# Shifted weight units and another order of splits in a three-product float32 decoder trunk

## Chip, cores and metric

The kernel runs on one core of a Trainium2 chip. The metric is the device time of one execution in microseconds (us); lower is better.

## The reference

Two decoder layers work on one sequence of 512 tokens with 1024 channels. Each layer is a half-step SwiGLU block, a mixer (gated linear attention with pooling in layer 0, top-k attention in layer 1) and a second half-step SwiGLU block; a last norm follows. So there are four SwiGLU blocks, and they hold most of the arithmetic:

```python
def swiglu(x, wi, wo):
    gate, up = jnp.split(x @ wi, 2, axis=-1)
    return (jax.nn.silu(gate) * up) @ wo
...
for li in range(DEPTH):
    h = h + 0.5 * swiglu(rms_norm(h, ffn1_norm[li]), ffn1_wi[li], ffn1_wo[li])
    hn = rms_norm(h, mix_norm[li])
...
    h = h + mix
    h = h + 0.5 * swiglu(rms_norm(h, ffn2_norm[li]), ffn2_wi[li], ffn2_wo[li])
return rms_norm(h, final_norm)
```

Here `wi` is 1024 x 5632 and `wo` 2816 x 1024, all in float32.

## The kernel before

**Products.** Every float32 operand of a large product is split into a high part (a copy to the type fp32r, by ScalarE) and a low part (the rest, by VectorE). `mm3` (L277 to 281) then issues three matmuls for each pair of 128 x 128 weights and moving tile: high by high (L279), high by low and low by high. In the blocks the weights are the stationary operand and the activations move. Most products have 512 moving columns. In the blocks' "seven products" (`seven_products`, L596 to 674), a 2 x 2 block scheme with seven products in place of eight, they have 256: 12 matmuls to a product, 84 to one of the 22 column groups `f` of a block. Also of 256 columns are the mixers' value products (bank `v`, 288 matmuls in all, where the weights move and the activations are stationary) and the output product of the odd mixer (bank `oo`, 384).

**Blocks.** `ffn(i, ...)` (L384) runs block i = 0 to 3. Its first groups `f` (four in block 0, three in the others, table `PLAIN`) are plain products of 512 columns; the others are seven products. The 22 groups are cut into three thirds (`THIRDS`: 8, 7, 7); each third ends with an output stage over m = 0 to 7 (bank `o`, 512 columns, 3 x 7 or 3 x 8 matmuls to each m).

**Weights.** A weight chunk is loaded by SP's DMA queue into one of two buffers `src0` and `src1`, in turn (`emit_load`, L214), and is split from there into units. There are four units, each a pair of tiles `u0h, u0l` to `u3h, u3l`; a unit can be written again when the products that read it have ended. A plain chunk takes two units for its two halves. A chunk of seven products takes unit 0 for `ab`, unit 1 for `z` and unit 2 or 3 (in turn) for `ds`; VectorE first adds blocks of the raw chunk together (L682, L691, L693). In its products `ab` is read first, then `ds`, then `z`.

```python
def unit_tile(u, off, name):
    n = (UNIT if u < 2 else UNIT + S) + UPAD
    return tuple(wpool.tile([P, n], F32R, tag=f"u{u}{x}", name=f"u{x}_{name}")[:, off:n] for x in "hl")
```

`off` counts columns of 4 bytes: the unit's data begin `off` columns into its tile. The unit tiles begin 160 bytes past a multiple of 256, and the moving tiles of the blocks (`hgh`, `hgl`, `th`, `tl`) 96 bytes past one. With off = 48 (192 bytes) a unit therefore begins at 96 too, and moving and stationary tiles lie at a **distance** of 0 (moving address less stationary address, modulo 256 bytes); all products of 512 columns with weights stand at 0. The table `SHIFT` gives the seven products another `off` in each third of each block, so another distance:

| block | distance in its thirds (bytes) |
|---|---|
| 0 | 192, 160, 128 |
| 1 | 96, 64, 32 |
| 2 | 0, 224, 176 |
| 3 | 240, 208, 80 |

The `v` and `oo` products stand at 192.

**Order.** In `ffn` the work is recorded as tasks with an engine, an assumed duration and dependencies; `Schedule.run` (L94) plays them through and emits each engine's instructions in the order that comes out. PE and SP keep the order in which tasks were added; ScalarE and VectorE follow the assumed times. Each engine then works strictly through its list. Lines 406 to 410 stand for what is under way when a block begins: the loads of its third and fourth chunk land after 3 and 5 us, the first products wait 5 us (`begun`), and in block 0 VectorE is busy for 20 us. `load_up_to` takes a load for 2.4 us per 1024 columns.

Of the kernel before, what the change touches and what calls it, by code (L numbers as in the profile page):

```python
# [17 lines left out]
P = 128  # L18
# [6 lines left out]
THIRDS = ((0, 8), (8, 15), (15, 22))  # L25

PLAIN = ((0, 1, 2, 3), (0, 1, 2), (0, 1, 2), (0, 1, 2))

SHIFT = ((0, 8, 16), (24, 32, 40), (48, 56, 4), (52, 60, 28))
UNIT = 1024  # L30
UPAD = 64
RANK = 16
EPS = 1e-6
# [109 lines left out]
def trunk(ctx, tc, xT, pos, wi, wo, wev, walr, gw, pw, wevo, wod, wodx, wodo, cst, cident, cperm, cscan, clev, ccaus,  # L143
# [24 lines left out]
    def chunk(kind, src, n, eng=V, units=(0, 1), off=0):  # L168
        chunks.append((kind, src, n, eng, units, off))

    def ffn_chunks(i):
        for t, (fa, fb) in enumerate(THIRDS):
            for f in range(fa, fb):
                if f in PLAIN[i]:
                    chunk("P", wi[i, f], 2048, units=(2, 3) if f % 2 else (0, 1), off=48)
                else:
                    chunk("S", wi[i, f], 2048, off=SHIFT[i][t])
            for m in range(0, KD, 3):
                n = (fb - fa) * P
                c0 = fa * KD * P + m * n  # L180
                chunk("O", wo[i, :, c0:c0 + min(3, KD - m) * n], min(3, KD - m) * n)

    def mix_chunks(them):
        for n, (src, eng, off) in enumerate(them):
            chunk("C", src, src.shape[-1], eng, ((0, 1), (2, 3))[n % 2], off)

    ffn_chunks(0)
    EVEN0 = len(chunks)
    chunk("A", walr, KD * RANK)
    mix_chunks([(wev[c], G if c > 1 else V, 32 if c in (2, 3) else 48) for c in range(8)]  # L190
               + [(wevo[c], V if c > 1 else G, 0) for c in range(4)])
    ffn_chunks(1)
    ffn_chunks(2)
    mix_chunks([(wod[0], V, 48), (wodx, V, 48)]
               + [(wod[c], V if c == 6 else G, 32 if c == 6 else 48) for c in range(1, 7)]
               + [(wodo[c], V if c > 1 else G, 0) for c in range(4)])
    ffn_chunks(3)
    parts = {}
# [185 lines left out]
    def ffn(i, next_gain, rope_steps=None):  # L384
        last_ffn = next_gain is None
        with tc.tile_pool(name=f"ffn{i}", bufs=1) as fp, tc.tile_pool(name=f"ffnt{i}", bufs=2) as ft:
# [17 lines left out]


            for n in (2, 3):
                loaded[at["use"] + n] = add("SP", (3.0, 5.0)[n - 2], lambda: None)
            begun = add("SP2", 5.0, lambda: None)
            if i == 0:
                add("DVE", 20.0, lambda: None).late = -1.0  # L410


            def load_up_to(c):
                while at["load"] <= min(c, len(chunks) - 1):
                    n = at["load"]
                    loaded[n] = add("SP", 2.4 * chunks[n][2] / 1024, lambda n=n: emit_load(n), src_free[n % 2])
                    src_free[n % 2] = []
                    at["load"] += 1

# [139 lines left out]
            def plain_products(f, t, c, w, tls, rest):  # L559
                gp, up = new_bank("g"), new_bank("u")  # L560
                d = {"third": t}
                units = chunks[c][4]
                for q in range(4):
                    def mms(q=q):
                        w_ = w()
                        for k in (2 * q, 2 * q + 1):
                            for s, rec in enumerate((gp, up)):
                                mm3(ps_of(rec), col(w_, k * 256 + s * P, k * 256 + (s + 1) * P), hg[k],
                                    k == 0, k == KD - 1)
                    tp = add("PE", 12 * 0.2267, mms, tls[q // 2] if tls else None,  # L570
                             (gp["after"], up["after"]) if q == 0 else None, begun if f == 0 else None)
                    readers[units[q // 2]].append(tp)
                    if rest and q < 3:
                        rest.pop(0)()
                    if i == 0 and f == 1 and q == 1:
                        add_norm()
                if f == 0:
                    if i > 0:
                        add_norm()
                    add_blocks()  # L580

                def gate():
                    d["g"] = ft.tile([P, S], F32, tag="g", name=f"g{f}")
                    V.tensor_tensor(d["g"], ps_of(gp), R, op=ALU.mult)

                def evac():
                    t1 = add("DVE", dve_us(S) + 0.06, gate, tp, state["norm"], g_ring[-2:-1])
                    gp["free"].append(t1)
                    t2 = add("ACT", act_us(S), lambda: A.activation(d["g"], d["g"], AF.Silu), t1)
                    silus.append(t2)  # L590
                    t3 = add("DVE", dve_us(S) + 0.06, lambda: V.tensor_tensor(d["g"], ps_of(up), d["g"], op=ALU.mult), t2)
                    up["free"].append(t3)
                    act_out(f, d, t3)
                return evac
# [104 lines left out]

            wo_parts, wo_tl = {}, {}  # L700

            def out_split(m, nb, c):
                load_up_to(c)
                u = m % 4
                held = wo_parts[m] = []
                wo_tl[m] = split_part(c, u, held, (m % 3) * nb * P, nb * P, loaded.get(c))

# [6 lines left out]
            def out_task(rec, m, t, j0, j1):  # L714
                fa, fb = THIRDS[t]
                held = wo_parts[m]
                tp = add("PE", (j1 - j0) * 3 * 0.2267, lambda: out_mms(ps_of(rec), held, t, j0, j1), wo_tl[m],
                         rec["after"] if j0 == 0 else None, [acts[fa + j] for j in range(j0, j1)])
                readers[m % 4].append(tp)
                return tp  # L720

            def scaled(m, ps, a=0, b=S):
# [4 lines left out]
            def out_end(rec, m, t, tp):  # L727
                x = add("DVE", 2 * dve_us(S) + 0.06, lambda: scaled(m, ps_of(rec)), tp, up_ring[-2:-1])
                up_ring.append(x)
                rec["free"].append(x)  # L730
                if t < 2:
                    return
                if not last_ffn:
                    gc = cs[:, C_GAIN[next_gain] + m:C_GAIN[next_gain] + m + 1]
                    y = add("ACT", act_us(S), lambda: post_hi(m, next_gain), x)
                    add("DVE", dve_us(S) + 0.03, lambda: post_lo(m, next_gain), y)
                else:
                    add("ACT", act_us(S), lambda: final_copy(m), x)
                y = add("ACT", act_us(S), lambda: square_a(m), x, state.get("sqs", [])[-2:-1])
                if m > 0:  # L740
                    state.setdefault("sqs", []).append(
                        add("DVE" if m == KD - 1 else "POOL", 0.7 if m == KD - 1 else 1.5,
                            lambda: square_b(m, V if m == KD - 1 else G), y, state.get("sqs", [])[-1:]))

# [27 lines left out]
            for t, (fa, fb) in enumerate(THIRDS):  # L772
# [30 lines left out]
                for m in range(KD):  # L803
                    if m % 3 == 0:
                        c = at["use"]
                        at["use"] += 1
                        at["split"] += 1
                    out_split(m, nb, c)
                    if m % 3 == 2 or m == KD - 1:
                        load_up_to(c + 2)  # L810
                    if m >= whole:
                        continue
                    rec = new_bank("o")
                    if m == 0:

                        tp = out_task(rec, m, t, 0, 3)
                        if pending:
                            pending.pop(0)()
                        tp = out_task(rec, m, t, 3, nb - 3 if pending else nb - 1)
                        if pending:  # L820
                            pending.pop(0)()
                            tp = out_task(rec, m, t, nb - 3, nb - 1)
                        held_back = rec
                        if rope_steps and t < 2:
                            dep = tp
                            for fn in rope_steps["ia"[t]]:
                                dep = add("DVE", 1.0, fn, dep)
                        continue
                    if m == 1:
                        tp = out_task(rec, m, t, 0, nb - 1)  # L830
                        out_end(held_back, 0, t, out_task(held_back, 0, t, nb - 1, nb))
                        tp = out_task(rec, m, t, nb - 1, nb)
                    else:
                        tp = out_task(rec, m, t, 0, nb)
                    out_end(rec, m, t, tp)
# [547 lines left out]
    def odd_mixer():  # L1383
        with tc.tile_pool(name="od", bufs=1) as od, tc.tile_pool(name="odt", bufs=2) as ot:
            caus = od.tile([P, P], F32, name="caus")
            nc.sync.dma_start(caus, ccaus)
            qki = od.tile([P, 4 * S], F32, tag="x8", name="qki")
            qi = [qki[:, 0:S], qki[:, S:2 * S]]
            ki = qki[:, 2 * S:3 * S]
# [403 lines left out]
```

## Time and profile before

| | us |
|---|---|
| median of 3 runs | 1792.13 (1785.35 to 1794.0) |
| the profiled execution | 1793.27 |
| its span, first to last instruction | 1791.5 |
| TensorE matmul busy | 1755.9 (98%) |
| TensorE weight loads busy | 1571.2 (88%) |
| VectorE busy | 1360.0 (76%) |
| ScalarE busy | 860.7 (48%) |

The time outside the span is 1.8 us. Matmuls are pipelined and the ends of their records are modelled: a 256-column matmul is shown with 280 ns although the next one begins some 0.12 us later. How fast they run is therefore read from the distance between starts, or from the number of matmuls in a stretch of known length (one or two in each count began before the stretch).

### The profile page before, as it was taken

The page shows a single profiled execution, that of the slowest core. Times are in us where ns is not written, and L with a number is a line of the kernel's source. Part 1 is how long each engine was busy: PE and PEld are TensorE (multiplying, and loading weights), DVE is VectorE, ACT ScalarE, POOL GpSimd, SP SyncE. Part 2 cuts the span into 40 slices and gives each one's busy share as a digit, 9 for nine tenths or more (in the row PEclk, how much of TensorE's full clock was granted, in tenths as well). Part 3 has the DMA queues.
Part 4 walks back from the last instruction along what each step waited for, and adds up shares of the span by engine and source line. Part 5 has one row for each costly group of instructions (what it writes and reads, how often), then busy time and mean ns, then how long its engine had stood idle before and what let it go on. Part 6 is the DMA issues. An engine that isn't in the chain of part 4 may idle for free.

```text
span 1791.5 us, 27132 instructions
## 1 busy us (share of the span) xinstructions
PE 1755.9 (98%) x11102; PEld 1571.2 (88%) x11102; DVE 1360.0 (76%) x1876; ACT 860.7 (48%) x1296; POOL 196.6 (11%) x175
## 2 busy tenths in 40 slices
PE   9999999999999999999999999999999999999997
PEld 6989999888687989999889898998687989898996
DVE  7968778749467778888877696876996577686875
ACT  6525536443355535446555253454455455253453
POOL 0000000235320000000100000002574200000002
PEclk9999999999999999999999999999999999999998
DMA  5323323222122322323313233232220223233231
GB/s 190 116 74 96 122 81 131 97 84 71 48 74 74 134 79 95 130 87 118 111 62 132 71 113 112 95 106 89 71 88 32 95 69 121 71 118 106 88 113 48
DMA packets 37629, 170.45 MB, mean 95 GB/s; under 512 B 4320, under 2 KB 7296, under 8 KB 29440
## 3 DMA queue, kind: packets, MB, share of 16 engines
q1 hardware_dynamic: 37504, 168.72, 28.1%
q8 instruction: 87, 1.43, 0.3%
q14 instruction: 38, 0.31, 0.1%
HBM read 166.60 MB, written 2.10 MB: 94 GB/s over the span
## 4 chain that ended last, share of the span: by engine, by line
PE 85%; DVE 8%; issue 2%; ACT 2%; DMA 2%; POOL 1%; SPq 0%; DVEq 0%; POOLq 0%; ACTq 0%
PE o L279 9%; PE o L281 9%; PE o L280 9%; PE a L281 8%; PE a L279 8%; PE a L280 8%; PE bc L281 6%; PE bc L279 6%; PE bc L280 6%; PE pj L279 2%; PE pj L280 2%; PE pj L281 2%; DMA src<-in_wi_dram 2%; DVE ul L446 1%; PE oo L280 1%
## 5 line engine op out<-in xcount | busy, mean ns | idle before, releaser
L444 ACT ACTIVATE uh<-src 128x1024 fp32r<-128x1024 f32 (+2 forms) x321 | 362.9, 1137 | 436.4 <-PE o L280 232.2
L446 DVE TENSOR_TENSOR ul<-src,uh 128x1024 fp32r<-128x1024 f32 (+2 forms) x321 | 420.8, 1318 | 40.4 <-ACT uh L444 28.9
L279 PE MATMUL o<-acth,uh 128*128 128x512 f32 (+1 forms) x718 | 276.8, 386 | 0.0
L281 PE MATMUL o<-acth,ul 128*128 128x512 f32 (+1 forms) x718 | 276.6, 385 | 0.0
L280 PE MATMUL o<-actl,uh 128*128 128x512 f32 (+1 forms) x718 | 276.6, 385 | 0.0
L279 PE MATMUL a<-th,uh 128*128 128x256 f32 x900 | 253.6, 282 | 0.0
L281 PE MATMUL a<-th,ul 128*128 128x256 f32 x900 | 253.0, 281 | 0.0
L280 PE MATMUL a<-tl,uh 128*128 128x256 f32 x900 | 252.8, 281 | 0.0
L755 POOL TENSOR_TENSOR acc<-acc,sq 128x512 f32<-128x512 f32 x23 | 30.8, 1341 | 1368.0 <-ACT sq L752 1368.0
L279 PEld LDWEIGHTS a<-th,uh 128*128 128x128 f32 x900 | 169.7, 189 | 2.7 <-DVE up L661 2.0
L280 PEld LDWEIGHTS a<-tl,uh 128*128 128x128 f32 x900 | 170.0, 189 | 0.7
L279 PE MATMUL bc<-hgh_f,uh 128*128 128x256 f32 x600 | 170.3, 284 | 0.0
L281 PE MATMUL bc<-hgh_f,ul 128*128 128x256 f32 x600 | 170.2, 284 | 0.0
L280 PE MATMUL bc<-hgl_f,uh 128*128 128x256 f32 x600 | 170.1, 284 | 0.0
L281 PEld LDWEIGHTS a<-th,ul 128*128 128x128 f32 x900 | 169.7, 189 | 0.0
L281 PEld LDWEIGHTS o<-acth,ul 128*128 128x128 f32 x718 | 134.9, 188 | 27.3
L280 PEld LDWEIGHTS o<-actl,uh 128*128 128x128 f32 x718 | 134.9, 188 | 25.6
L279 PEld LDWEIGHTS o<-acth,uh 128*128 128x128 f32 x718 | 134.9, 188 | 25.6
L724 DVE SCALAR_TENSOR_TENSOR o<-o,R 128x512 f32<-128x512 f32 (+1 forms) x98 | 66.4, 677 | 92.3 <-PE o L281 91.8
L682 DVE TENSOR_TENSOR src<-src 128x1024 f32<-128x1024 f32 x75 | 91.7, 1223 | 55.7 <-DMA src<-in_wi_dram 55.6
L280 PEld LDWEIGHTS bc<-hgl_f,uh 128*128 128x128 f32 x600 | 115.0, 192 | 0.0
L279 PEld LDWEIGHTS bc<-hgh_f,uh 128*128 128x128 f32 x600 | 114.7, 191 | 0.1
(345 smaller groups left out, 3919.0 us busy)
## 6 DMA issues: line engine op xcount, KB each, us to landing
src<-in_wi_dram SPq DMA_DIRECT2D x150, 512.0 KB, 4.3
src<-in_wo_dram SPq DMA_DIRECT2D x16, 1344.0 KB, 5.7
src<-in_wi_dram SPq DMA_DIRECT2D x12, 1024.0 KB, 4.9
src<-in_wo_dram SPq DMA_DIRECT2D x8, 1536.0 KB, 6.2
src<-in_wev_dram SPq DMA_DIRECT2D x8, 1024.0 KB, 4.8
src<-in_wo_dram SPq DMA_DIRECT2D x8, 896.0 KB, 4.5
src<-in_wod_dram SPq DMA_DIRECT2D x7, 1024.0 KB, 4.8
src<-in_wo_dram SPq DMA_DIRECT2D x4, 1024.0 KB, 4.9
```

Source lines behind the costliest of these rows:

```text
L279: T.matmul(ps, st[0], mv[0], start=start, stop=False, skip_group_check=on)
L280: T.matmul(ps, st[0], mv[1], start=False, stop=False, skip_group_check=on)
L281: T.matmul(ps, st[1], mv[0], start=False, stop=stop, skip_group_check=on)
L444: A.activation(held[0], raw, AF.Copy)
L446: tl = add("DVE", dve_us(n), lambda: V.tensor_tensor(held[1], raw, held[0], op=ALU.subtract), th)
L682: V.tensor_tensor(src[:, 1536:2560].rearrange("p (s c) -> p s c", s=2), src.rearrange("p (s c) -> p s c", c=S)[:, 2:6:3], cc[:, None, :].t ...
L724: V.scalar_tensor_tensor(x[:, a:b], ps[:, a:b], 0.5, R[:, a:b], op0=ALU.mult, op1=ALU.mult)
L755: eng.tensor_tensor(acc, acc, sq_tiles[m], op=ALU.add)
```

## The change

Seven edits, in the order of the diff:

- The table `SHIFT` is dropped; all seven products use off = 32 (128 bytes). Their stationary tiles then begin at 160 + 128 = 288, which is 32 past a multiple of 256, and the distance is 96 - 32 = 64 bytes in every third.
- Plain chunks take units (2, 3) in the first and the third of three groups, and (0, 1) in the second; before it was (0, 1), (2, 3), (0, 1). In block 0, with four, they stay as they were. The mixers' chunks begin with (2, 3) in place of (0, 1).
- The `v` chunks get off = 0 in place of 32, and a tile of 128 bytes is put ahead of the odd mixer's tiles; `v` and `oo` then stand at a distance of 64 too. With these all 6,972 matmuls of 256 columns of the seven, `v` and `oo` products stand at 64.
- In the last output stage of a block, m = 4 to 7 use units 2, 3, 0, 1 in place of 0, 1, 2, 3.
- What is under way at a block's begin is assumed differently: the two loads land after 0 and 8 us, `begun` goes, ScalarE and VectorE are busy for 5 us (20 in block 0), in block 0 PE for 6 us.
- A load is taken for 1.0 us + 2.3 us per 1024 columns.
- The list of squares (`state["sqs"]`) begins with m = 0.

```diff
-SHIFT = ((0, 8, 16), (24, 32, 40), (48, 56, 4), (52, 60, 28))
 UNIT = 1024
+
+OUT_UNITS = (0, 1, 2, 3, 0, 1, 2, 3)
+OUT_LAST = (0, 1, 2, 3, 2, 3, 0, 1)
...
-                    chunk("P", wi[i, f], 2048, units=(2, 3) if f % 2 else (0, 1), off=48)
+                    chunk("P", wi[i, f], 2048, units=(0, 1) if (len(PLAIN[i]) - f) % 2 == 0 else (2, 3), off=48)
                 else:
-                    chunk("S", wi[i, f], 2048, off=SHIFT[i][t])
+                    chunk("S", wi[i, f], 2048, off=32)
...
-            chunk("C", src, src.shape[-1], eng, ((0, 1), (2, 3))[n % 2], off)
+            chunk("C", src, src.shape[-1], eng, ((2, 3), (0, 1))[n % 2], off)
...
-    mix_chunks([(wev[c], G if c > 1 else V, 32 if c in (2, 3) else 48) for c in range(8)]
+    mix_chunks([(wev[c], G if c > 1 else V, 0 if c in (2, 3) else 48) for c in range(8)]
...
-               + [(wod[c], V if c == 6 else G, 32 if c == 6 else 48) for c in range(1, 7)]
+               + [(wod[c], V if c == 6 else G, 0 if c == 6 else 48) for c in range(1, 7)]
...
-                loaded[at["use"] + n] = add("SP", (3.0, 5.0)[n - 2], lambda: None)
-            begun = add("SP2", 5.0, lambda: None)
+                loaded[at["use"] + n] = add("SP", (0.0, 8.0)[n - 2], lambda: None)
+            for eng in ("DVE", "ACT"):
+                add(eng, 20.0 if i == 0 else 5.0, lambda: None).late = -1.0
             if i == 0:
-                add("DVE", 20.0, lambda: None).late = -1.0
+                add("PE", 6.0, lambda: None)
...
-                    loaded[n] = add("SP", 2.4 * chunks[n][2] / 1024, lambda n=n: emit_load(n), src_free[n % 2])
+                    loaded[n] = add("SP", 1.0 + 2.3 * chunks[n][2] / 1024, lambda n=n: emit_load(n), src_free[n % 2])
...
-                             (gp["after"], up["after"]) if q == 0 else None, begun if f == 0 else None)
+                             (gp["after"], up["after"]) if q == 0 else None)
...
-                u = m % 4
+                u = (OUT_LAST if t == 2 else OUT_UNITS)[m]
...
-                if m > 0:
-                    state.setdefault("sqs", []).append(
+                if m == 0:
+                    state["sqs"] = [y]
+                else:
+                    state["sqs"].append(
...
+            od.tile([P, 32], F32, name="shift0")
```

No engine has an instruction more or less, and PE, SP and POOL keep their order. On ScalarE and VectorE instructions move; three places matter below.

ScalarE, the begin of block 1, before: `uh_47` are the high parts of the first seven-product chunk (f = 3; 2560 is `ab`, 0 is `z`, 1024 is `ds`), `uh_48` those of the next; `g0` to `g2` and `acth0`, `acth1` are the gates and activations of the plain groups f = 0 to 2.

```order
L444 ACTIVATE uh_47_1024_5069<-src1_73 128x1536
L589 ACTIVATE g0_5055<-g0_5055 128x512
L549 ACTIVATE acth0_5089<-g0_5055 128x512
L444 ACTIVATE uh_48_1024_5107<-src0_72 128x1536
L589 ACTIVATE g1_5110<-g1_5110 128x512
L549 ACTIVATE acth1_5128<-g1_5110 128x512
L444 ACTIVATE uh_47_2560_5144<-src1_73 128x1024
L444 ACTIVATE uh_47_0_5173<-src1_73 128x1024
L589 ACTIVATE g2_5176<-g2_5176 128x512
```

The same place now:

```order
L446 ACTIVATE uh_47_2560_5045<-src1_73 128x1024
L526 ACTIVATE th2_4901<-tsa2_5048 128x512
L529 ACTIVATE th2_4901<-tsb2_5051 128x512
L501 ACTIVATE b12_3_5073<-h3_79,cs_87 128x256
L591 ACTIVATE g0_5071<-g0_5071 128x512
L446 ACTIVATE uh_47_0_5093<-src1_73 128x1024
L526 ACTIVATE th3_4902<-tsa3_5075 128x512
L529 ACTIVATE th3_4902<-tsb3_5096 128x512
L551 ACTIVATE acth0_5103<-g0_5071 128x512
L446 ACTIVATE uh_47_1024_5134<-src1_73 128x1536
L591 ACTIVATE g1_5138<-g1_5138 128x512
L551 ACTIVATE acth1_5158<-g1_5138 128x512
```

`ab` and `z` of f = 3 moved from behind the activation of f = 1 to ahead of the gate of f = 0 and the activation of f = 0; `ds` is now the last of the three. Blocks 2 and 3 show the same.

ScalarE, the last output stage of block 0, before: `uh_29` are the splits for m = 3 (0), 4 (896) and 5 (1792), `uh_30` those for m = 6 (0) and 7 (896).

```order
L444 ACTIVATE uh_29_0_3201<-src1_73 128x896
L549 ACTIVATE acth21_3224<-g21_3158 128x512
L444 ACTIVATE uh_29_896_3235<-src1_73 128x896
L444 ACTIVATE uh_29_1792_3263<-src1_73 128x896
L349 ACTIVATE hgh0_mix_0_3267<-h0_76,cs_87 128x512
```

The same place now:

```order
L446 ACTIVATE uh_29_0_3201<-src1_73 128x896
L551 ACTIVATE acth21_3224<-g21_3158 128x512
L446 ACTIVATE uh_30_0_3235<-src0_72 128x896
L446 ACTIVATE uh_30_896_3263<-src0_72 128x896
L753 ACTIVATE acc_84<-h0_76 128x512
L350 ACTIVATE hgh0_mix_0_3270<-h0_76,cs_87 128x512
L756 ACTIVATE sq1_3274<-h1_77 128x512
L350 ACTIVATE hgh1_mix_0_3276<-h1_77,cs_87 128x512
L446 ACTIVATE uh_29_896_3305<-src1_73 128x896
L756 ACTIVATE sq2_3312<-h2_78 128x512
```

The splits for m = 6 and 7 went ahead of those for m = 4 and 5; the one for m = 4 now stands behind the post-work of m = 0 and 1.

## Rows read from the trace of the kernel before

**Rows 1.** The page: busy time by engine, and the chain's shares by engine.

```profile
PE 1755.9 (98%) x11102; PEld 1571.2 (88%) x11102; DVE 1360.0 (76%) x1876; ACT 860.7 (48%) x1296; POOL 196.6 (11%) x175
...
PE 85%; DVE 8%; issue 2%; ACT 2%; DMA 2%; POOL 1%; SPq 0%; DVEq 0%; POOLq 0%; ACTq 0%
```

**Rows 2.** Timeline of PE in block 1, second third: start, shown duration, instruction.

```profile
699.95 0.28 PE L279 MATMUL a<-th,uh 128*128 128x256 f32 x1
...
700.29 0.28 PE L279 MATMUL a<-th,uh 128*128 128x256 f32 x1
```

**Rows 3.** Stretches, PE alone, one per third: length, busy (instructions), clock, DMA share, GB/s.

```profile
54.00:90.00 36.00, 35.01 (x297) 1.00 0.42 146
140.00:200.00 60.00, 60.00 (x508) 1.00 0.31 102
250.00:310.00 60.00, 60.00 (x507) 1.00 0.39 124
585.00:628.00 43.00, 43.00 (x357) 0.99 0.39 138
680.00:740.00 60.00, 59.99 (x529) 1.00 0.39 134
785.00:845.00 60.00, 60.00 (x517) 1.00 0.34 115
930.00:973.00 43.00, 43.00 (x357) 0.99 0.41 143
1025.00:1085.00 60.00, 60.00 (x508) 1.00 0.38 127
1133.00:1193.00 60.00, 60.00 (x507) 1.00 0.33 110
1465.00:1508.00 43.00, 43.00 (x358) 0.98 0.41 142
1560.00:1620.00 60.00, 59.86 (x486) 1.00 0.35 113
1670.00:1730.00 60.00, 60.00 (x511) 1.00 0.33 108
```

**Rows 4.** Stretches, PE alone: the even mixer's `v`, the odd mixer's `oo`.

```profile
384.40:401.40 17.00, 17.00 (x147) 1.00 0.19 64
1392.00:1422.00 30.00, 30.00 (x257) 1.00 0.32 106
```

**Rows 5.** Waits of PE: us in total, times, longest.

```profile
PE a L279 <- ACT uh L444: 9.0, 3, 3.6
...
PE a L281 <- DVE ul L446: 2.7, 4, 1.0
```

**Rows 6.** Stretches, PE alone: the first 10 us of seven products in blocks 1 to 3.

```profile
575.60:585.60 10.00, 5.94 (x26) 0.68 0.22 63
922.80:932.80 10.00, 7.20 (x45) 0.83 0.34 105
1456.70:1466.70 10.00, 6.28 (x27) 0.66 0.26 76
```

**Rows 7.** Timeline of ScalarE at that point of block 1; in brackets idle time before.

```profile
577.50 0.63 ACT L549 ACTIVATE acth<-g 128x512 fp32r<-128x512 f32 x1 [2.23 <-DVE g L591]
578.04 1.99 ACT L444 ACTIVATE uh<-src 128x1024 fp32r<-128x1024 f32 x2
```

**Rows 8.** Stretches, all engines: one third of block 1, one output stage.

```profile
680.00:740.00 60.00, 59.99 (x529) 59.99 (x530) 51.91 (x63) 35.89 (x56) 0.00 (x0) 1.00 0.39 134
...
100.00:130.00 30.00, 30.00 (x134) 24.82 (x134) 21.46 (x26) 6.56 (x7) 0.00 (x0) 1.00 0.23 71
```

**Rows 9.** Timelines of ScalarE and VectorE, last output stage of block 0.

```profile
331.70 0.94 ACT L444 ACTIVATE uh<-src 128x896 fp32r<-128x896 f32 x1
...
331.30 0.68 DVE L724 SCALAR_TENSOR_TENSOR o<-o,R 128x512 f32<-128x512 f32 x1
...
333.04 1.08 DVE L446 TENSOR_TENSOR ul<-src,uh 128x896 fp32r<-128x896 f32 x1
```

More of the change, by code (lines that the diff above doesn't have):

```diff
@@ L700, in ffn, with out_split @@
             wo_parts, wo_tl = {}, {}
-            def out_split(m, nb, c):
+            def out_split(m, nb, c, t):
                 load_up_to(c)
-                u = m % 4
+                u = (OUT_LAST if t == 2 else OUT_UNITS)[m]
                 held = wo_parts[m] = []
@@ L718, in out_task @@
                          rec["after"] if j0 == 0 else None, [acts[fa + j] for j in range(j0, j1)])
-                readers[m % 4].append(tp)
+                readers[(OUT_LAST if t == 2 else OUT_UNITS)[m]].append(tp)
                 return tp
@@ L807, in ffn @@
                         at["split"] += 1
-                    out_split(m, nb, c)
+                    out_split(m, nb, c, t)
                     if m % 3 == 2 or m == KD - 1:
```

## The prediction

> **What bounds the kernel now.** I read the page first: matmuls cover 98% of the span, and 85% of the chain that ended last lies on PE [rows 1]. VectorE has 76%, the DMA queues far less. So time is saved only where PE runs through its list faster or waits less. The list itself stays: no matmul goes or comes.
>
> How fast PE runs is not in the durations but in the starts. In the second third of block 1 the same form returns after three matmuls, 700.29 - 699.95 = 0.34 us, 113 ns to a 256-column matmul [rows 2]. Then I counted the matmuls in one stretch of seven products in each third [rows 3]. The work there is the same; only the distance between moving and stationary tiles differs. At 64 bytes 529 ran in 60 us, 113.4 ns each. No other distance does as well: 116.1 ns at 32, 117.4 at 80, 118.1 at 160 and at 224, 118.3 at 128 and at 176, 117.9 at 192 (its idle time left out), 120 at 96, 0 and 240, 123.5 at 208. The granted clock is 1.00 in the long stretches, 0.98 or more in all (1.00 is the 2.4 GHz level), and PE is shown busy throughout, so the difference is not a wait for another engine's result.
>
> Then the waits of PE. Its largest are three for ScalarE's `uh`, together 9.0 us [rows 5]: the begin of the seven products in blocks 1 to 3. In the first 10 us there PE ran 26, 45 and 27 matmuls, at a mean granted clock of 0.68, 0.83 and 0.66 [rows 6]: it had stood idle, and went on at the lower level (1.2 GHz) for a while.
>
> **Part A, the distance.** All seven products, `v` and `oo` go to 64 bytes. I take 113.4 ns for each and sum, per third, number times (pace now - 113.4). Block 0, 336 matmuls in the first third, pace 35.01 / 297 = 117.9 (its idle time left out): 1.5 us; then 588 x 4.7 = 2.8 and 588 x 4.9 = 2.9. Block 1: 420 x 7.0 = 2.9; the second third is there already, 0; 588 x 2.7 = 1.6. Block 2: 2.9, 2.8, 2.9. Block 3: 420 x 6.7 = 2.8, 588 x 10.1 = 5.9, 588 x 4.0 = 2.4. Together 31.4 us. The `oo` products run at 30 / 257 = 116.7 and `v` at 17 / 147 = 115.6 ns [rows 4]: 384 x 3.3 = 1.3 and 288 x 2.2 = 0.6. **A = 33.3 us.** Since PE is the bound and the order of its list stays, all of it is on the path, if VectorE keeps up: at 113.4 ns it was busy 51.91 of 60 us [rows 8], so it does.
>
> The Trainium skill speaks against this part. "TensorE: Matmul & The Clock Gate", in "Step-by-step: what each phase is for", has two independent read ports, one for the moving operand and one for weight loads, and says: "Loading the next tile's weights doesn't steal SBUF read bandwidth from the running matmul." By that rule where the two lie should not matter, and A would be 0. The stretches of rows 3 speak against it here, but a distance was measured once for most values, so the rule remains as a rival below.
>
> **Part B, the begin of the blocks.** Before, f = 2 used units 0 and 1, and `ab` of f = 3 needs unit 0. Its high part stood in ScalarE's list behind the activation of f = 1, which itself waited 2.23 us for VectorE; `uh` began at 578.04 [rows 7], well after the last plain matmul. Now f = 2 holds units 2 and 3, `ab` and `z` are split while f = 2 runs, and only `ds`, which the third product reads first, waits for half of f = 2. PE gives that third product 2 x 12 matmuls = 2.7 us more; the splits of `ds` behind it need, by their width, some 1.99 / 2 x 1.5 = 1.5 us on ScalarE [rows 7] and 1.08 x 1536 / 896 = 1.9 us on VectorE [rows 9], and the other half of f = 2 lasts about 5.4 us (24 matmuls of 30 / 134 = 0.224 us, rows 8). So the cover is 5.4 + 2.7 = 8.1 us for 3.4 us of work.
>
> What this is worth: at 113.4 ns PE would run 88 matmuls in 10 us. It lacks 62, 43 and 61 [rows 6], 166 x 0.1134 = 18.8 us, of which 0.7 us is the pace that part A has counted (98 matmuls by 7 ns). Block 0 already has the new units, since its fourth plain group uses 2 and 3; its first stretch was busy 35.01 of 36 us [rows 3], so about 1 us of idle time is left with them. I leave 3 x 1 us. **B = 18.8 - 0.7 - 3.0 = 15.1 us.** The bounds are 0 (the wait comes back elsewhere) and 18.1.
>
> **Part C, the units of the last output stage.** m = 4 now needs unit 2, which m = 2 has just left, with only m = 3 between (21 matmuls x 0.224 = 4.7 us); before there were three. ScalarE, VectorE and then PE are queued behind it. The chain can be read in the stage as it is: m = 2 was evacuated from 331.30, and the split that stood behind it ended at 333.04 + 1.08 = 334.12 [rows 9], 2.8 us. The same for m = 5 after m = 3. So 1.9 us is spare: 0. If the cover were gone, each of the 8 places would cost at most what a whole begin of block 1 cost, 62 x 0.1134 = 7.0 us.
>
> **The rest** costs nothing. Where the order within a third changes, PE can gain no more than its waits for VectorE's `ul`, 2.7 us [rows 5]; a loss is hidden by the 8.1 us in 60 that VectorE has free. The 128 bytes ahead of the odd mixer and the list of squares add no instruction. The load's assumed time changes VectorE's order alone, since SP's order stays, and a chunk can only be asked for earlier where its buffer is split earlier.
>
> **Sum.** 1793.3 (the profiled execution) - 33.3 - 15.1 = 1744.9 us. That execution lies 1.1 us above the median of the runs, so the median to expect is **1744 us**.
>
> **Rivals.**
>
> - *The begin of the blocks still waits*, because the new order only moves the wait, say to `ds` of f = 4, which now needs unit 3 when f = 2 has ended. For it: ScalarE's list there is full of waits for VectorE [rows 7]. Against it: 8.1 us of cover. Time: 1793.3 - 33.3 - 1.1 = 1759 us. Chance 0.14.
> - *The pace has nothing to do with the distance* (the rule above): the stretch at 64 was fast for something else in that third. For it: `v` and `oo` at one distance, 192, run at 115.6 and 116.7 ns, while the third at 192 needs 117.9, so something else moves the pace by 2 ns. Against it: 32 and 80, next to 64, are the second and third best of the thirds. Time: 1793.3 - 15.1 - 1.1 = 1777 us. Chance 0.05.
> - *The last output stage waits at all its 8 places* (part C), from the point where the chain of 2.8 us is late by more than 1.9 us, as it would be if VectorE evacuated m = 2 behind other work. At 7.0 us each this is 56 us: 1744 + 56 = 1800 us. Chance 0.02, and half of it for the half as many places, 1772 us.
> - *The place of a unit alone sets the pace*, and off = 32 is a bad one once all thirds have it. From a mean of 118.4 + 15.1 / 6.3 = 120.8 ns in the seven products on, the kernel is slower than before; at the slowest pace of rows 3, 123.5 ns, 6300 x 5.1 = 32 us are lost against 15.1 gained: 1792 + 17 = 1809 us. Against it: the one third with off = 32 is the fastest. Chance 0.02.
> - That the edits don't do what they say can be put aside: the tile sizes give the distance of 64, and the order is shown above.
>
> **How the numbers follow.** The forecast has what is left, 0.77. Its own range: all of B's bound, and the 2.7 us of the rest, give 1793.3 - 33.3 - 18.1 - 2.7 - 1.1 = 1738; a pace of 115 ns in place of 113.4 costs 6972 x 1.6 = 11 us, 1755. I let the range begin at 1735, for a mixer or a first block that gains a little too, and end at 1761, so that it holds the first rival; outside lie the others, about 0.1 with the tails. A measurement of this kernel can tell about 0.5%, 9 us, from no change: the runs before lie within 9 us. Faster by more: the forecast, the first two rivals and half of the third, 0.96; within: the rest of the third and a share of the fourth, 0.02; slower: 0.02.
>
> **What would show it.** Right: some 527 or more matmuls in 60 us of every third, also in the third that had 486; no wait of PE for `uh` at the begin of blocks 1 to 3, and there a granted clock near 1.00 and 80 or more matmuls in 10 us; no wait of PE in the last output stages. Wrong: paces near 118 ns at a distance of 64 (part A), or a low granted clock where a block's seven products begin (part B).

## The result, and the profile after

The changed kernel takes **1761.15 us** (median of 4 runs, 1758.91 to 1766.73), against 1792.21 (1785.35 to 1794.0, 4 runs) for the kernel before: ratio 0.9838, 95% interval 0.9804 to 0.9873. It is faster, by 31 us where 48 were forecast; 1761.15 lies 0.15 us outside the range. The profiled execution took 1761.35 us, its span is 1759.6.

The page, busy time by engine and the chain's shares, against [rows 1]: 20.6 us less of TensorE, the same instructions, and 92% of the chain on PE.

```profile
PE 1735.3 (99%) x11102; PEld 1552.9 (88%) x11102; DVE 1356.7 (77%) x1876; ACT 858.4 (49%) x1296; POOL 197.4 (11%) x175
...
PE 92%; DVE 4%; issue 1%; POOL 1%; DMA 1%; ACT 1%; SPq 0%; DVEq 0%; ACTq 0%; POOLq 0%
```

The waits of PE, against [rows 5], the longest of them (us in total, times, longest). The wait of 9.0 us for `uh` at the begin of blocks 1 to 3 is gone, and no output stage (bank `o`) has taken its place; what is left stands at the kernel's start (`g`), its end (`st`) and in the mixers.

```profile
PE lg L1492 <- DVE qki L1430: 3.4, 1, 3.4
PE st L338 <- ACT sq L866: 2.9, 1, 2.9
PE g L280 <- ACT uh L270: 1.8, 1, 1.8
```

Stretches, PE alone: the first 10 us of seven products in blocks 1 to 3, against [rows 6] (length, busy with instructions, granted clock, DMA share, GB/s). 26, 45 and 27 matmuls have become 87, 86 and 88, at a clock of 1.00 in place of 0.68, 0.83 and 0.66.

```profile
572.80:582.80 10.00, 10.00 (x87) 1.00 0.29 102
912.40:922.40 10.00, 10.00 (x86) 1.00 0.22 86
1437.60:1447.60 10.00, 10.00 (x88) 1.00 0.33 105
```

Stretches, PE alone, one in each third, against [rows 3]. All stand at a distance of 64 bytes now. The forecast wanted 527 or more in every 60 us. Four thirds have that (250, 670, 1010, 1535); the other eight have 511 or 512 in 60 us, 306 in 36 or 367 in 43: 117 to 118 ns, no better than most distances gave before.

```profile
54.00:90.00 36.00, 36.00 (x306) 1.00 0.44 147
140.00:200.00 60.00, 60.00 (x512) 1.00 0.32 105
250.00:310.00 60.00, 60.00 (x530) 1.00 0.39 134
575.00:618.00 43.00, 43.00 (x367) 1.00 0.39 134
670.00:730.00 60.00, 60.00 (x532) 1.00 0.40 134
775.00:835.00 60.00, 60.00 (x512) 1.00 0.34 116
912.50:955.50 43.00, 43.00 (x367) 1.00 0.37 130
1010.00:1070.00 60.00, 60.00 (x532) 1.00 0.40 134
1115.00:1175.00 60.00, 60.00 (x511) 1.00 0.35 117
1438.00:1481.00 43.00, 43.00 (x367) 1.00 0.41 138
1535.00:1595.00 60.00, 60.00 (x531) 1.00 0.39 134
1640.00:1700.00 60.00, 60.00 (x512) 1.00 0.35 117
```

Where the time went, from the distance between successive starts of PE's matmuls in the two profiled executions (1793.3 and 1761.35 us): in the products of three matmuls those of 256 columns (the 6,972 and 84 of bank `o` at the kernel's end) sum to 851.7 before and 827.0 after, of which steps over 160 ns hold 16.7 and 5.5 us more than matmuls at pace would; those of 512 columns sum to 843.5 and 836.1 (the waits ahead of `uh` stand here, behind the last plain matmul). So about 11 + 7 us came from the waits and the low clock at the begin of the blocks, and 24.7 - 11.2 = 13.5 us from the pace, where the forecast had 15.1 and 33.3.

What the four fast thirds have in common is seen at their begin. The timeline of PE at 1008 us (block 2, second third; start, shown duration, instruction) and the weight load at the jump (in brackets idle time and who ended it):

```profile
1008.32 0.28 PE L280 MATMUL bc<-th,uh 128*128 128x256 f32 x1
1008.44 0.28 PE L281 MATMUL bc<-tl,uh 128*128 128x256 f32 x1
1008.86 0.39 PE L282 MATMUL bc<-th,ul 128*128 128x256 f32 x1
1009.08 0.28 PE L280 MATMUL bc<-th,uh 128*128 128x256 f32 x1
1009.20 0.28 PE L281 MATMUL bc<-tl,uh 128*128 128x256 f32 x1
1009.31 0.28 PE L282 MATMUL bc<-th,ul 128*128 128x256 f32 x1
...
1008.86 0.19 PEld L282 LDWEIGHTS bc<-th,ul 128*128 128x128 f32 x1 [0.35 <-DVE ul L448]
```

The third begins with 26 matmuls at 117.9 ns. Then the weight load waits 0.35 us for the low part of `ds` (VectorE, L448), the next starts lie 0.42 and 0.22 us apart, and from there on the third runs at 113.3 ns to its end. The other three fast thirds read the same; the eight slow ones have no wait. A wait stands where the first seven product's `ds` takes unit 3, which m = 7, the last of the output stage ahead of it, has only just left; unit 2 is free after m = 6. The kernel before has the same in its one third at 64 bytes, 20 us ahead of [rows 2]:

```profile
679.50 0.28 PE L279 MATMUL bc<-th,uh 128*128 128x256 f32 x1
679.61 0.28 PE L280 MATMUL bc<-tl,uh 128*128 128x256 f32 x1
680.01 0.38 PE L281 MATMUL bc<-th,ul 128*128 128x256 f32 x1
680.23 0.28 PE L279 MATMUL bc<-th,uh 128*128 128x256 f32 x1
```

So the pace of 113.4 ns on which part A rests came behind a wait. That gave the theory to test: **a distance of 64 bytes has two paces, 117.8 and 113.3 ns, and a short wait can switch from the first to the second**; a fast third is worth 537 x 4.5 ns = 2.4 us. Rivals: the pace belongs to the place or the data of the third; a wait alone does it, whatever the distance.

### The profile page after: what moved, and what is told of

It is laid out like the page before. It is cut to its first block, busy times and chain, and to the rows that moved or that the text cites. A ratio compares the mean times of both kernels' runs of the same rounds, so it can differ in the third digit from the quotient of the medians.

```text
span 1759.6 us, 27138 instructions
## 1 busy us (share of the span) xinstructions
PE 1735.3 (99%) x11102; PEld 1552.9 (88%) x11102; DVE 1356.7 (77%) x1876; ACT 858.4 (49%) x1296; POOL 197.4 (11%) x175
## 4 chain that ended last, share of the span: by engine, by line
PE 92%; DVE 4%; issue 1%; POOL 1%; DMA 1%; ACT 1%; SPq 0%; DVEq 0%; ACTq 0%; POOLq 0%
PE o L282 9%; PE o L281 9%; PE o L280 9%; PE a L281 8%; PE a L280 8%; PE a L282 8%; PE bc L282 6%; PE bc L281 6%; PE bc L280 6%; PE pj L280 2%; PE pj L282 2%; PE pj L281 2%; PE g L282 1%; PE g L281 1%; PE u L281 1%
## 5 line engine op out<-in xcount | busy, mean ns | idle before, releaser
L448 DVE TENSOR_TENSOR ul<-src,uh 128x1024 fp32r<-128x1024 f32 (+2 forms) x321 | 423.9, 1327 | 53.7 <-ACT uh L446 33.9
L282 PEld LDWEIGHTS bc<-hgh_f,ul 128*128 128x128 f32 x600 | 112.5, 187 | 0.0
```

Of the source, the lines that this page charges most:

```text
L282: T.matmul(ps, st[1], mv[0], start=False, stop=stop, skip_group_check=on)
L448: tl = add("DVE", dve_us(n), lambda: V.tensor_tensor(held[1], raw, held[0], op=ALU.subtract), th)
```

## The experiments

Each ratio is to the kernel before on the same chip. Paces are means of the distances between starts.

**Waits taken away (e1) and put elsewhere (e2, e3).** The unit that the first `ds` of a third takes is set ahead of each third: e1 always unit 2, e2 unit 3 in the second and third, e3 unit 3 in all.

```diff
+                at["ds"] = 0             # e1
+                at["ds"] = min(t, 1)     # e2
+                at["ds"] = 1             # e3
```

> The first seven product of every third takes unit 2 for ds. Unit 2 is left by m = 6 of the output stage before, unit 3 only by m = 7, so the short wait of PE for the low part of ds near the begin of a third should be gone in all thirds. Theory 1 (at a distance of 64 bytes the 256-column matmuls have two paces, 117.8 and 113.3 ns, and it is such a wait that throws PE from the slow into the fast one, which then lasts to the end of the third): all twelve thirds run at about 117.8 ns; four thirds lose 537 x 4.5 ns = 2.4 us each and get 0.4 us of waiting back, so about 8 us more than the changed kernel, 1769 us. Theory 2 (the pace belongs to the third itself, to its addresses or what runs beside it): the four fast thirds stay at 113.3 ns, time 1.6 us less, 1759.5 us.

> The first seven product of the second and the last third of every block takes unit 3 for ds, so that PE waits for it shortly in all eight. Theory 1: all eight at about 113.3 ns after the wait, the four first thirds at 117.8; four more thirds gain 2.4 us each and wait 0.4 us, about 8 us less than the changed kernel, 1753 us. Theory 2: the paces stay as they are, the four waits cost 1.6 us, 1763 us.

> As the run before, and the first thirds begin with unit 3 too, which the third plain group leaves only with its end, so that PE should wait there for about 1 us. Theory 1: all twelve thirds fast after the wait; the first thirds gain (309 + 3 x 393) x 4.5 ns = 6.7 us against some 4 us of waits, so 1750 us. If a longer wait leaves the pace slow, 1757 us. Theory 2: 1767 us.

e1: 1765.62 us (1762.41 to 1770.45), ratio 0.9846 (0.9811 to 0.9882). The waits at the begin of thirds are gone, and all four fast thirds with them: 117.8 ns. The first third of block 3, slow in the changed kernel, went to 113.3 behind its 49th matmul, at a single step of 185 ns. e2: 1760.40 (1757.13 to 1763.02), ratio 0.9814 (0.9781 to 0.9847); six of the eight thirds with a wait are fast, where all eight were expected. e3: 1763.66 (1758.46 to 1772.33), ratio 0.9838 (0.9796 to 0.9881); seven of twelve, the three long waits (steps of 0.9 to 2.2 us) among the five that failed. The three were expected at 1769, 1753 and 1750 us; their times came out closer together, and their intervals overlap each other and the changed kernel's. So the test rests on the paces, which were read on one chip. The rows are of PE alone, e1's block 0 third 3 and block 1 third 2, then the same two of e2:

```profile
250.00:310.00 60.00, 60.00 (x512) 1.00 0.35 117
667.00:727.00 60.00, 60.00 (x512) 1.00 0.34 117
```

```profile
250.00:310.00 60.00, 60.00 (x532) 1.00 0.41 135
666.00:726.00 60.00, 60.00 (x532) 1.00 0.39 134
```

So the fast pace goes and comes with the waits, against the rival of the place; but a wait is not sufficient, and the step of 185 ns shows that another short interruption can do it too.

**The order alone (e4).** Units, output stages and assumed times as changed, distances as before.

```diff
+SHIFT = ((0, 8, 16), (24, 32, 40), (48, 56, 4), (52, 60, 28))
-                    chunk("S", wi[i, f], 2048, off=32)
+                    chunk("S", wi[i, f], 2048, off=SHIFT[i][t])
```

> The changed kernel with the old distances: part B alone. If part B is worth what the begin of the blocks shows (18.8 us) and the distance 64 only its slow pace and the waits, 1773 us, and no wait for the high parts of ab at the begin of blocks 1 to 3. Rival (the distance brought all that was gained): 1790 us or more.

1773.28 us (1770.84 to 1774.31), ratio 0.9885 (0.9847 to 0.9922): parts B and C together are worth about 20 us, the forecast had 15.1. Waits with a step of 0.4 us stood at 128, 224 and 208 bytes too and gave 118.7, 118.3 and 117.8 ns; the third at 64 had its wait (395 and 221 ns) and this time stayed at 117.8. The edit keeps the units, the order of the last stage and the assumed times together, so it doesn't say which of them is worth how much.

**The same program again (e5, e10, e13), and the kernel before again (e11).** Nothing is edited.

> The changed kernel as it is, profiled a second time. In its first profile four of twelve thirds ran at 113.3 ns to a 256-column matmul (block 0 third 3, blocks 1 to 3 third 2), each from a wait of PE for the low part of ds on; the other eight ran at 117.8. Theory (the wait switches the pace, and how long it is decides it): the same waits stand in the same four thirds; which of them switch may differ by one or two, each worth 0.0045 us x 561 = 2.5 us, so 1757 to 1767 us. Rival (the pace belongs to the third, by its data or its place): the same four thirds to the matmul.

> The changed kernel, profiled a third time; four thirds were fast the first time, one the second. If the length of the wait decides and differs between executions: between none and four thirds at 113.3 ns, always among the four with a wait, and only where the two long steps read 422 or 423 and then 221 to 223 ns; 1772 us less 2.5 for each. If the chip decides (the second profile came from another one than the first): as the second, one third, 1770 us.

> The kernel before, profiled a second time. The prediction took 113.4 ns from its one third at 64 bytes (block 1, second). If that pace came from the wait and not from the distance, it may read 117.8 ns here (510 in 60 us in place of 529), with second long step of 224 ns or more; if the distance gives it, 113.4 again. The third at 32 bytes without a wait: 116.7 again either way.

> The changed kernel again, to see its times on the chip on which e12 and e14 run. Theory (each execution draws anew at four waits, 2.5 us each): times spread over some 10 us between executions of one program, 1760 to 1772 us. If a chip or a build fixed it, all its executions would agree within 0.3%, 5 us.

The same four thirds, in a stretch of 60 us each, first in e5 (1769.71 us), then in e10 (1766.2):

```profile
250.00:310.00 60.00, 60.00 (x532) 1.00 0.40 134
672.00:732.00 60.00, 60.00 (x512) 1.00 0.38 129
1012.00:1072.00 60.00, 60.00 (x512) 1.00 0.39 130
1542.00:1602.00 60.00, 60.00 (x512) 1.00 0.39 133
```

```profile
250.00:310.00 60.00, 60.00 (x512) 1.00 0.38 130
670.00:730.00 60.00, 60.00 (x511) 1.00 0.35 120
1010.00:1070.00 60.00, 60.00 (x512) 1.00 0.37 131
1540.00:1600.00 60.00, 60.00 (x512) 1.00 0.35 125
```

Four fast thirds in the first profile, one in e5, none in e10, four again in e13: one program, one set of addresses, another outcome. This also rules out the place. e13 took 1761.91 us (1756.64 to 1763.12, ratio 0.9836, 0.9817 to 0.9855); its profiled execution, with all four, was its fastest. Its five runs on one chip spread over 6.5 us: less than the 10 of the theory, more than the 5 of a fixed outcome. The kernel before, again (e11), had its third at 64 fast once more; that was luck, as e4 and e10 show.

The kernel before also shows that a wait can turn the pace the other way. Its slowest third in [rows 3], at 208 bytes (486 in 60 us), ran at 118.3 ns up to a wait of this kind and at 123.3 behind it. Behind the same wait it ran at 117.8 in e4 and in e11, whose row is:

```profile
1555.00:1615.00 60.00, 60.00 (x511) 1.00 0.37 128
```

What tells a wait that switches from one that doesn't is nanoseconds. Over all profiles there are 50 waits with a step of under 0.5 us at the begin of a third at 64 bytes (the steps are read in the records' own nanoseconds; the rows above round them to 10). Where the step behind the waiting matmul took 221 to 223 ns, 30 of 34 thirds were fast; where it took 224 to 229, none of 16. That step lies behind the wait, so it may be part of the outcome already; what decides it isn't shown.

One rival was not tested: the chip. The profiles come from several chips, and the share of these waits that switched is not the same on them: 13 of 17 and 9 of 11 on the chips of e1 to e4 and of e12 to e14, 2 of 12 and 1 of 5 on those of e5 to e8 and of e9 to e11, 5 of 5 in the first two profiles. Each of the four chips shows both outcomes, so the chip doesn't fix them; but no chip is on record with two profiles of one program, and whether the chip shifts the odds stays open.

e10 is faster than e5 although it has a fast third less. The even mixer explains most of that: from 420 to 460 us the mean clock that the chip granted differs between executions of one program. PE alone, e5 and then e13; e10 reads nearly as e13 (196 matmuls), the first profile as e5. 175 against 194 matmuls, most of 512 columns, are 19 x 0.227 = 4.3 us.

```profile
420.00:460.00 40.00, 37.23 (x175) 0.87 0.23 79
```

```profile
420.00:460.00 40.00, 37.23 (x194) 1.00 0.23 79
```

**The waits at another distance (e6).** As e2, with off = 16.

```diff
-                    chunk("S", wi[i, f], 2048, off=32)
+                    chunk("S", wi[i, f], 2048, off=16)
+                at["ds"] = min(t, 1)
```

> As e2 (unit 3 first in every second and third third, so a wait stands in eight thirds), but all seven products at a distance of 128 bytes in place of 64. Theory (a wait gives the fast pace only at some distances, 64 among them): no third runs at 113.3 ns, all near 118.7; with e2's 1760 as base, six thirds of 561 matmuls lose 5.4 ns and the rest 0.9 ns: 18 + 2.6 = 21 us more, about 1781 us. Rival (a wait alone gives the fast pace, at any distance): as e2, 1757 to 1763 us.

1779.92 us (one run): as the theory had it, and against the rival that a wait alone is enough. Eight waits stood there and no third settled below 118.6 ns. The eight began at about 118.5; behind the wait three went up to 120.0 and five stayed at 118.7. Of the four without a wait three ran at 120.0, and one went from there to 118.7 at a step of 162 ns. So 128 has two paces too, 1.3 ns apart.

**The distance alone (e7).** The kernel before with off = 32, the new places of `v` and `oo`, and nothing else.

```diff
-                    chunk("S", wi[i, f], 2048, off=SHIFT[i][t])
+                    chunk("S", wi[i, f], 2048, off=32)
...
+            od.tile([P, 32], F32, name="shift0")
```

> The kernel before with the distance of 64 in all 256-column products and nothing else (units, order and assumed times as before): part A alone. The prediction's step (113.4 ns for each at 64) gives 1794 - 33 = 1760 us. Theory (117.8 ns without a wait, 113.3 behind some waits): PE's time in 256-column products goes down by about as much as between the kernel with the order alone and the changed kernel, 840 - 827 = 13 us, so about 1781 us, with three to seven thirds at 113.3 ns. The waits for uh at the begin of blocks 1 to 3 stay, 9 us as before.

1789.05 us (1779.98 to 1791.61, 10 runs), ratio 0.9979 (0.9961 to 0.9997). Part A by itself is worth 0.21%, 3.8 us (by the interval 0.5 to 7), not 33, and not the 13 of my own theory either: in the profiled execution four thirds began with a short wait, and one became fast (block 3 second). 3.8 us is what a steady 117.8 ns gives: the kernel before has a mean of 118.35 ns over its steps under 160 ns, and 6972 x 0.55 = 3.8. The waits for `uh` are as before.

```profile
PE a L279 <- ACT uh L444: 8.8, 3, 3.4
```

**The products of 512 columns at 64 bytes too (e8).**

```diff
-                    chunk("P", wi[i, f], 2048, units=(0, 1) if (len(PLAIN[i]) - f) % 2 == 0 else (2, 3), off=48)
+                    chunk("P", wi[i, f], 2048, units=(0, 1) if (len(PLAIN[i]) - f) % 2 == 0 else (2, 3), off=32)
...
-                chunk("O", wo[i, :, c0:c0 + min(3, KD - m) * n], min(3, KD - m) * n)
+                chunk("O", wo[i, :, c0:c0 + min(3, KD - m) * n], min(3, KD - m) * n, off=48)
```

> The changed kernel with the products of 512 columns at a distance of 64 bytes too (they stand at 0). Open question: whether the pace of a 512-column matmul depends on the distance at all. If the same 2 to 7 ns per matmul are to be had, about 3,500 of them give 7 to 25 us: 1736 to 1754 us. If not, 1761 us as the changed kernel. If 0 is the good distance for 512 columns, slower, up to 1775 us.

1774.99 us (1772.46 to 1782.69), ratio 0.9917 (0.9886 to 0.9947): slower. A 512-column matmul takes 230.2 ns on average at 64 against 227.4 at 0, some 3,450 x 2.8 = 9.7 us; the first output stage of a block shows it best, with 130 in 30 us where there are 134 at 0 [rows 8]. Part of the 14 us is the draw: in the profiled execution, its slowest (1782.69), none of the four waits switched.

```profile
100.00:130.00 30.00, 30.00 (x130) 1.00 0.22 71
```

**A scan (e9).** e1 with another distance in every third and output stage.

```diff
+SCAN7 = ((44, 36, 20), (12, 38, 42), (34, 30, 46), (39, 41, 32))
+SCANO = ((56, 60, 4), (8, 16, 24), (32, 40, 52), (62, 2, 12))
-                    chunk("S", wi[i, f], 2048, off=32)
+                    chunk("S", wi[i, f], 2048, off=SCAN7[i][t])
+                at["ds"] = 0
```

> The kernel of e1 (unit 2 first, so that no third begins with a wait) with another distance in each third's seven products (block 0: 16, 48, 112; block 1: 144, 40, 24; block 2: 56, 72, 8; block 3: 36, 28, 64 bytes) and in each output stage of 512 columns (32, 16, 240; 224, 192, 160; 128, 96, 48; 8, 248, 208). Theory (64 is no optimum: the steady pace depends weakly on the distance, between 116.7 ns at 32 and 120 at 0 in the runs so far): every third between 116 and 120 ns, those next to 32 (24 to 48) near 117, and 117.8 at 64 again. Rival (some distance runs at 113.3 steadily): one third at 113.3 from its first matmul on. The 512-column stages: 227.4 ns at 0 and 230.2 at 64 so far; open at the others.

1785.17 us (one run). No distance runs at 113.3 steadily. Paces without a wait: 116.7 ns at 48 bytes; 117.3 at 16, 117.6 at 8, 117.8 at 24, 64 and 72; 120.0 at 28, 40, 56, 112 and 144; 120.7 at 36. The guess that the neighbours of 32 do well failed for 28, 36 and 40. The rows are the stretches at 48, 40 and 64:

```profile
140.00:200.00 60.00, 60.00 (x516) 1.00 0.33 109
672.00:732.00 60.00, 60.00 (x503) 1.00 0.33 107
1662.00:1722.00 60.00, 60.00 (x512) 1.00 0.33 110
```

For 512 columns 0 stays the best beside 16 (227.1 ns); the others read 230.7 to 234.1.

**48 bytes everywhere (e12), e2 again (e14), and 48 without waits (e15).**

```diff
-                    chunk("S", wi[i, f], 2048, off=32)
+                    chunk("S", wi[i, f], 2048, off=36)     # e12, e15
+                at["ds"] = min(t, 1)                       # e14
+                at["ds"] = 0                               # e15
```

> The changed kernel with its seven products at 48 bytes in place of 64. e9 measured 116.7 ns there, steadily, in one third without a wait (117.8 at 64). If that pace holds in all thirds and no wait switches it: 6300 x 1.1 = 6.9 us less than the changed kernel without fast thirds, so 7 us below e13's slowest runs and about as fast as e13's runs with three fast thirds. If the four waits switch it as at 64, each takes another 561 x 3.4 = 1.9 us off. If the one third was an accident like the one the prediction read at 64: 117 to 120 ns in the others, 1765 to 1780 us.

> e2 again (eight waits in place of four; six thirds were fast in its first profile), beside e13 on one chip. If a wait is switched to the fast pace more often than not: 2 to 4 more fast thirds, 5 to 10 us less, minus 8 waits of 0.4 = 3 us, so 2 to 7 us below e13. If on this chip the waits seldom switch, as in e5, e8 and e10: equal to e13 or up to 2 us above it.

> e12 (48 bytes) with e1's order of units (unit 2 first in each third), so that the four waits of 0.4 us go as well. At 48 bytes a wait buys nothing: e12 less 4 x 0.4 = 1.6 us, 1758.7 us if run on e12's chip, with executions as close together as e12's (0.5 us). If removing the waits brings others (as it did in no third of e1), 1760 us or more.

e12: 1760.34 us, four runs from 1759.9 to 1760.42, ratio 0.9828 (0.9809 to 0.9846). All twelve thirds run at 116.7 ns and none of the four waits switched anything. Block 0 third 2, block 1 thirds 2 (with its wait) and 3:

```profile
138.00:198.00 60.00, 60.00 (x517) 1.00 0.32 110
...
664.00:724.00 60.00, 59.85 (x513) 1.00 0.36 121
770.00:830.00 60.00, 60.00 (x517) 1.00 0.34 113
```

e14: 1758.29 us (1757.49 to 1758.94), ratio 0.9817 (0.9798 to 0.9835), five of eight waits switched; 3.6 us below e13 on the same chip, in the middle of the 2 to 7 expected, though its profile has one fast third more than e13's and not two to four. e15: 1761.29 us (1759.64 to 1763.16), ratio 0.9828 (0.9815 to 0.9842), the same twelve thirds at 116.7 ns. The four waits are gone, and the 256-column steps sum to 828.4 us against 830.1 in e12, 1.7 us less where 1.6 were expected; the time doesn't show it. This was another chip, and the profiled execution had a clock of 0.87 in the even mixer (e12: 0.96). So no version is clearly ahead of the changed kernel: 0.9817 and 0.9828 against 0.9838 and 0.9836, with intervals that overlap. e12's four runs lie closest together (0.5 us; e15's, at the same paces, 3.5), and e2 is the lowest in both of its measurements.

## Why the prediction was wrong

- **Part A was the step that failed: "At 64 bytes 529 ran in 60 us, 113.4 ns each ... I take 113.4 ns for each".** The count was right and its reading wrong. 113.4 was the pace of one third behind one wait. Without a switch, 64 bytes give 117.8 ns, and A is worth 3.8 us (e7, 0.9979); each third that switches adds 2.4. In the first profile four did: 3.8 + 4 x 2.4 = 13.4, against the 13.5 found above. That the result ended so near the range is owed to them, which is luck: e5, with one, took 1769.71 us.
- "PE is shown busy throughout, so the difference is not a wait for another engine's result" was true of the stretch and missed what stood ahead of it: the 0.32 us wait of a weight load at 680 us lay just where the stretch begins. The timeline from the begin of the third would have shown 117.9 ns up to the wait and 113.3 from it on.
- The second rival, "so something else moves the pace by 2 ns", was right in its conclusion and wrong in its figures. The counts of [rows 4] hold two matmuls each that began before the stretch: 145 `v` and 255 `oo` begin inside, 117.8 ns apart, as the third at 192 does. The clue lies elsewhere in the trace of before: three groups of 24 `v` or `oo` products run at 113.5 to 114.0 ns and the others at 117.6 to 118.0, all at 192 bytes. In e11 the last eleven such groups of `oo` ran at 113.3. That rival got 0.05 and 1777 us. The result lies between it and the forecast.
- The rule beside that rival (the Trainium skill, "TensorE: Matmul & The Clock Gate", "Step-by-step: what each phase is for", two independent read ports) does not hold here as it was applied: the place does matter, 116.7 ns at 48 against 120.0 at 40 in one execution (e9), and 116.7 in all 24 thirds of e12 and e15. Its price for A, 0, was nearer all the same than mine.
- Two more paces of [rows 3] were misread. The 358 at 240 bytes hold eight steps of about 212 ns at the lower clock; the others lie 118.3 ns apart, not 120. The 123.5 at 208, worth 5.9 us in the sum, came behind a wait (e11: 117.8).
- **Part B was right in kind and some 3 to 5 us too small**: 15.1 forecast, 11.2 + 7.4 = 18.6 in the profile, about 20 in e4 (0.9885, so 14 to 27). The term that was off is the 3 x 1 us of idle time left at the begin: nothing is left, 86 to 88 matmuls in the first 10 us at a clock of 1.00. The cover of 8.1 us was enough; the rival that the wait comes back is refuted. That it was the new units, and not the new assumed times that move ScalarE's splits ahead, was argued and not tested apart.
- **Part C, 0, was right**: no wait of PE in the output stages. VectorE keeps up, also in the thirds at 113.3 ns.
- The forecast's own lower case "a pace of 115 ns in place of 113.4 costs 11 us" was the right term with too small a bound: the row of the third at 192, 117.9, was a bound from the trace for a pace without whatever made 64 fast, 6972 x 4.5 = 31 us.

The mechanism of the switch stays open: what in a wait of 0.35 us decides between the two paces was not found, nor whether the chip has a part in it, nor whether the distance or the place of the stationary tile counts, since only that tile was moved. The scatter has two shown parts: the fast thirds, and the clock in the even mixer.

## What to carry to other kernels

A pace read from one stretch is a sample of one: look at how the stretch begins, and at the same setting elsewhere, before multiplying it by thousands of matmuls. Where two settings differ by 4% in a back-to-back stream, profile the same program twice; if a stretch changes its pace with no edit, that pace can't be credited to a setting. For a short stretch take the distance between starts: a count there is off by the matmuls that began before it. Units chosen so that the last group before a change of form leaves the next form's first unit free, with the splits into it ordered early, are worth a whole stall and the low clock behind it, here 6 to 7 us at each of three places.

## What the hardware showed that was not expected

- A stream of 256-column matmuls at 64 bytes has two stable paces, 117.8 and 113.3 ns, for 500 matmuls and more on end; in the traces kept a third went from the first to the second only at a short interruption (a weight load late by 0.29 to 0.35 us, or one step of 185 ns). At 192 bytes the same two were seen: in e11 the first third of block 0 went from 117.8 to 113.3 at steps of 153 and 223 ns and stayed there; the kernel before did the same and was put back to 117.8 by a wait of 1.0 us. At 128 there are two as well, 120.0 and 118.7, at 32 in e11 116.7 and 117.8. At 48 bytes all 25 thirds of e9, e12 and e15 ran at 116.7, four of them behind a wait.
- The pace without an interruption depends on the distance, from 116.7 (48 bytes) to 120.7 ns (36). The 123.3 at 208 stood behind a wait; the same third read 117.8 in e4 and e11.
- 512 columns want another distance than 256: 227 ns at 0 and 16 bytes, 229 to 234 elsewhere.
- Of two executions of one program, on two chips, one had a mean granted clock of 0.87 for 40 us in the even mixer and one 1.00, with PE busy 37.23 of the 40 us in both: 4.3 us.
